# Block products at the openings of three networks and for the mixer's first eight units of a two-layer encoder trunk

## The chip, the cores and the metric

One Trainium2 chip, one core. A single launch computes the whole trunk. The metric is device time in microseconds (us), lower is better; the median of the runs counts.

The engines of a core run side by side: TensorE (PE) multiplies into PSUM, VectorE (DVE) and ScalarE (ACT) work elementwise, GpSimd (POOL) does a few elementwise operations and issues the DMAs that add in flight, and SyncE (SP) issues the plain loads. Each engine takes its instructions in order, and an instruction waits until the others have made what it needs.

## The reference

Two layers on 528 tokens (16 learned ones and 512 frames) of 1024 channels, all float32:

```python
for l in range(DEPTH):                       # 2
    h = h + 0.5 * swiglu(rmsnorm(h, g1[l]), w_gate1[l], w_up1[l], w_down1[l])   # 1024 -> 2816 -> 1024
    h = h + hybrid_mixer(rmsnorm(h, gm[l]), ...)
    h = h + 0.5 * swiglu(rmsnorm(h, g2[l]), w_gate2[l], w_up2[l], w_down2[l])
h = rmsnorm(h, final_norm)[:, N_META:]

def swiglu(x, wg, wu, wd): return (silu(x @ wg) * (x @ wu)) @ wd

def hybrid_mixer(u, ...):
    q, k, v, a, b, g_sb, g_conv = split(u @ w_in)     # 512 each, the gates 1024 each
    y_sb   = stick_breaking_attention(q, k, v) @ w_attn_out
    y_conv = silu(layernorm(depthwise_conv31(a * sigmoid(b)))) @ w_conv_out
    return (sigmoid(g_sb) * y_sb + sigmoid(g_conv) * y_conv) @ w_out
```

## The kernel before

Channels lie on the 128 partitions and tokens along the row: h is eight tiles of 128 x 528. To keep float32 accuracy every operand is a pair of a rounded high part and a low remainder, and every product is three matmuls: high by high, high by low, low by high. Tokens go as two halves of 264 (256 each where layer 1 has dropped the learned tokens, which the code calls XO).

**Units.** `units` (L130 on) lists the weight tiles in the order of use. A plain unit is one 128-column tile of a matrix, 8 blocks of 128 x 128: 8 x 3 x 2 = 48 matmuls. `unit` (L243) hands out the next and prepares three ahead (`LOOK`); `prep_unit` (L213) makes the pair `wh`, `wl`, four buffers of each. A network's tile is split by an ACT cast and a DVE subtraction (`split`, L77). A mixer's tile is cast on ACT, its negative written on ACT, and the low part made by a DMA that adds the weights once more (L224 to L226, POOL's queue). `fetch` (L179) loads raw tiles over SP's queue into three `wr` buffers, in the order of `fetches`.

**Block products.** Inside the networks most row pairs (m, m+1) of gate and up go by Strassen-Winograd (`quad`, L566): the 2 x 2 blocks of weights (two output rows by two halves of the channels) and of activations (two halves of the channels by two halves of the tokens) take seven products instead of eight, named w11, s1, s2, w21, s3, w22, s4. Each is 24 matmuls for gate and up together. The sums of weight blocks are loaded into `s1` and `s3` by a plain load and an adding DMA (`fetch_sums`, L196); s2 and s4 come out of s1 by one DVE addition (L236). The sums of activation blocks, `S[0]` to `S[3]`, come from `sums` (L365): two ACT copies, four DVE operations of half width, and two splits. The first three are made in the stage before (`prepare`, L313), the fourth in the head. Partial results are copied in PSUM (L599, L603) and subtracted by DVE (L608, L613).

**A network** (`ffn`, L467) opens with plain units, because its norm and the last sum are late: `head` (L517) does rows 0 and 1, four plain units, with the norm's matmuls (L409) inside the second; layer 0's first network has its own opening (`first_head`). Then quads and, in four groups, the down products (L260), which update h; the last group also makes the next stage's operands.

**A mixer** (`mixer`, L678) copies h to DRAM, then does units b and a in turn for four channel tiles (L761 to L774): b times the norm into a sigmoid, a times the norm, and their product `uc` on POOL. Products q, k, v and the gates follow (L720), with the attention between them. The causal convolution is 31 taps for each channel tile on DVE (L748), all of tile 0, then all of tile 1, and so on. `conv_some` puts them behind evictions at a late priority, two or four at a time; the last must be done before the layer norm's matmul (L1032), which stands behind the first attention-out unit (`AO_FIRST`).

Of the kernel before, what the change touches and what calls it, by code (L numbers as in the profile page):

```python
# [24 lines left out]
PLAIN, PLAIN_FIRST = 2, 4  # L25
# [8 lines left out]
CONV_STEP = 4  # L34
# [4 lines left out]
AO_FIRST = 1  # L39
# [21 lines left out]
def kernel(ctx, tc, hT, par, const, wg1, wu1, wd1, win, wao, wco, wout, wg2, wu2, wd2, out):  # L61
# [15 lines left out]
    def split(x, hi, lo):  # L77

        act.copy(hi, x)  # L79
        dve.tensor_tensor(out=lo, in0=x, in1=f(hi), op=ALU.subtract)  # L80

# [14 lines left out]
    def fn(out, in_, func, **kw):  # L96
# [8 lines left out]
        table["acts"].append(i)  # L105

# [3 lines left out]
    RAW_OF = {"w11": (0, 0), "w22": (1, 1), "w12": (0, 1), "w21": (1, 0)}  # L110
# [19 lines left out]
    units = []  # L130
    for l in range(DEPTH):
        for fi, (wg, wu, wd) in enumerate(((wg1, wu1, wd1), (wg2, wu2, wd2))):
            if fi == 1:
                for i in range(4):
                    units += [(("b", l, i), win[l, 16 + i], 8), (("a", l, i), win[l, 12 + i], 8)]
# [11 lines left out]
            m = PLAIN if l or fi else PLAIN_FIRST  # L147
            for m in range(m):
                units += [((f"g{fi}", l, m), wg[l, m], 8), ((f"u{fi}", l, m), wu[l, m], 8)]
            m += 1  # L150
# [8 lines left out]
    ready, raws, spared = {}, {}, set()  # L159
    quads = {"pool": None, "of": None}  # L160

    def pieces(n, block=None):

        key, src, nk = units[n]
        if nk in QUAD:
            wg, wu, m = src
            k, c = RAW_OF[block or nk]
            return [(4 * e, 4 * e + 4, w[m + c, :, 4 * k:4 * k + 4]) for e, w in enumerate((wg, wu))]
# [3 lines left out]
    fetches = []  # L172
    for n, (key, src, nk) in enumerate(units):
        if nk == "w11":
            fetches += [n, n + 5, n + 3]
        elif nk not in QUAD:
            fetches.append(n)

    def fetch(spare=None):  # L179

        while state["fetch"] < len(fetches) and (spare or state["out"] < RAW):
            n = fetches[state["fetch"]]
            state["fetch"] += 1
            if spare:
                raw = spare
                spared.add(units[n][0])
            else:
                state["out"] += 1
                raw = wpool.tile([P, 8, P], F32, tag="wr", bufs=RAW, name="wr")
            for a, b, src in pieces(n):  # L190
                nc.sync.dma_start(raw[:, a:b], src)
            raws[units[n][0]] = raw
            if spare:
                return

    def fetch_sums():  # L196

        n = state["sums"]
        while n < len(units) and units[n][2] != "w11":
            n += 1  # L200
        if n == len(units) or units[n][0][1:3] != quads["of"]:
            return
        state["sums"] = n + 1
        _, *at = units[n][0]
        for name, first in (("s1", "w11"), ("s3", "w22")):
            t = quads["pool"].tile([P, 8, P], F32, tag=name, bufs=2, name=name)
            for a, b, src in pieces(n, first):
                nc.sync.dma_start(t[:, a:b], src)
            for a, b, src in pieces(n, "w12"):
                pool.dma_start(t[:, a:b], src, accum_op=ALU.add)  # L210
            raws[(name, *at)] = t

    def prep_unit():  # L213
# [7 lines left out]
        if nk not in QUAD:  # L221
            raw = raws.pop(key)
            if key[0] in MIXER:
                act.copy(hi[:, :nk], raw[:, :nk])  # L224
                act.activation(lo[:, :nk], raw[:, :nk], AF.Copy, scale=-1.0)
                pool.dma_start(lo[:, :nk], src[:, :nk].bitcast(F32R), accum_op=ALU.add)  # L226
            else:
                split(raw[:, :nk], hi[:, :nk], lo[:, :nk])
            state["out"] -= key not in spared
        else:  # L230
            at = key[1:]
            if nk == "w11":
# [4 lines left out]
            split(raws[("s1" if nk in ("s2", "s4") else nk, *at)], hi, lo)  # L237
            for d in DONE[nk]:
                del raws[(d, *at)]
                state["out"] -= d in RAW_OF  # L240
# [36 lines left out]
    cc = cst.tile([P, N_CONST], F32, name="cc")  # L277
    ident = cc[:, C_ID:C_ID + P]
# [9 lines left out]
    def constants():  # L288

        nc.sync.dma_start(prm[:, N_NORM:], par[:, N_NORM:])  # L290
        nc.sync.dma_start(cc, const)
        with priority(LATE):
            dve.tensor_copy(trir, cc[:, C_TRI:C_TRI + P])
            dve.tensor_copy(l4, cc[:64, C_L4:C_L4 + P])
            dve.tensor_copy(l4[:, 95:96], cc[:64, C_L4 + 2 * P - 1:C_L4 + 2 * P])
# [853 lines left out]
```

## Time and profile before

| | |
|---|---|
| median of 3 runs | 2152.31 us |
| lowest and highest | 2151.03 and 2152.36 us |
| profiled execution, first to last instruction (span) | 2150.5 us |
| mean granted TensorE clock | 0.999 |
| DMA, mean | 151 GB/s, 324.90 MB |

The profile names a group of instructions by line, engine, operation and tile (out<-in), with its count, its busy time and the mean of one in ns, and then the idle time of the engine just before it and what ended that. The chain of waits is followed back from the last instruction; its rows are start and length in us. A row of busy time by window gives, for a stretch of the span, the busy time of each engine with the count of instructions in brackets. The profile's own time outside the span is not given; the median of the runs lies 1.8 us above it.

### The profile page before, as it was taken

The page shows a single profiled execution, that of the slowest core. Times are in us where ns is not written, and L with a number is a line of the kernel's source. Part 1 is how long each engine was busy: PE and PEld are TensorE (multiplying, and loading weights), DVE is VectorE, ACT ScalarE, POOL GpSimd, SP SyncE. Part 2 cuts the span into 40 slices and gives each one's busy share as a digit, 9 for nine tenths or more (in the row PEclk, how much of TensorE's full clock was granted, in tenths as well). Part 3 has the DMA queues.
Part 4 walks back from the last instruction along what each step waited for, and adds up shares of the span by engine and source line. Part 5 has one row for each costly group of instructions (what it writes and reads, how often), then busy time and mean ns, then how long its engine had stood idle before and what let it go on. Part 6 is the DMA issues. An engine that isn't in the chain of part 4 may idle for free.

```text
span 2150.5 us, 39932 instructions
## 1 busy us (share of the span) xinstructions
PE 2135.9 (99%) x16226; PEld 2052.8 (95%) x16226; DVE 1521.5 (71%) x2091; ACT 1137.9 (53%) x1587; POOL 488.7 (23%) x449
## 2 busy tenths in 40 slices
PE   9999999999999999999999999999999999999998
PEld 9999999999999999999999999999888889999897
DVE  7867685677766777677877676856677767767685
ACT  6434355467776545343554443554778775444354
POOL 1322321211111131313113223212112111322320
PEclk9999999999999999999999999999999999999999
DMA  8465536865578747464365655368656886665542
GB/s 236 133 165 141 142 104 198 181 138 119 134 169 180 175 129 189 129 161 122 99 169 145 168 140 146 103 193 184 142 127 133 187 188 167 159 175 143 144 111 77
DMA packets 140168, 324.90 MB, mean 151 GB/s; under 512 B 15568, under 2 KB 19664, under 8 KB 139984
## 3 DMA queue, kind: packets, MB, share of 16 engines
q1 hardware_dynamic: 101856, 226.36, 33.3%
q0 software_dynamic: 37440, 95.44, 26.1%
q8 instruction: 127, 2.08, 0.4%
q10 hardware_dynamic: 688, 0.55, 0.1%
q14 instruction: 57, 0.47, 0.1%
HBM read 315.86 MB, written 6.42 MB: 150 GB/s over the span
## 4 chain that ended last, share of the span: by engine, by line
PE 99%; ACT 0%; DVE 0%; DMA 0%; issue 0%; DVEq 0%; ACTq 0%
PE pb L580 16%; PE ps L580 16%; PE ps L720 15%; PE ps L260 12%; PE ps L706 10%; PE pe L260 6%; PE pb L260 6%; PE pe L580 5%; PE z L706 2%; PE ps L502 2%; PE pe L502 1%; PE pb L502 1%; PE z L877 1%; PE po L921 1%; PE z L900 1%; PE ps L554 1%
## 5 line engine op out<-in xcount | busy, mean ns | idle before, releaser
L79 ACT CAST wh<-wr 128x1024 fp32r<-128x1024 f32 (+4 forms) x275 | 242.2, 887 | 372.4 <-PE ps L260 94.5
L80 DVE TENSOR_TENSOR wl<-wr,wh 128x1024 fp32r<-128x1024 f32 (+4 forms) x275 | 300.6, 1096 | 57.4 <-ACT wh L79 53.5
L79 ACT CAST wh<-s 128x1024 fp32r<-128x1024 f32 x158 | 165.8, 1049 | 274.9 <-DVE s L236 83.1
L80 DVE TENSOR_TENSOR wl<-s,wh 128x1024 fp32r<-128x1024 f32 x158 | 216.1, 1368 | 59.4 <-ACT wh L79 58.7
L720 PE MATMUL ps<-uh,wh 128*128 128x264 f32 (+1 forms) x792 | 243.8, 308 | 0.0
L720 PE MATMUL ps<-uh,wl 128*128 128x264 f32 (+1 forms) x792 | 240.0, 303 | 0.0
L720 PE MATMUL ps<-ul,wh 128*128 128x264 f32 (+1 forms) x792 | 239.9, 303 | 0.0
L640 POOL TENSOR_TENSOR h<-h,dt 128x528 f32<-128x528 f32 (+1 forms) x96 | 179.9, 1879 | 258.1 <-DVE dt L638 255.2
L210 POOL DMA_DIRECT2D s<-wg x78 | 72.8, 938 | 596.9 <-DMA s<-wg 337.9
L748 DVE SCALAR_TENSOR_TENSOR y<-uc,prm,y 128x528 f32<-128x528 f32 (+1 forms) x240 | 197.7, 824 | 4.1
L224 ACT CAST wh<-wr 128x1024 fp32r<-128x1024 f32 x104 | 109.1, 1049 | 141.2 <-issue 46.9
L580 PE MATMUL ps<-ul,wh 128*128 128x264 f32 (+1 forms) x624 | 177.4, 284 | 0.0
L580 PE MATMUL pb<-sl,wh 128*128 128x264 f32 (+1 forms) x624 | 176.9, 283 | 0.0
L580 PE MATMUL ps<-uh,wl 128*128 128x264 f32 (+1 forms) x624 | 176.9, 283 | 0.0
L580 PE MATMUL pb<-sh,wl 128*128 128x264 f32 (+1 forms) x624 | 176.8, 283 | 0.0
L580 PE MATMUL pb<-sh,wh 128*128 128x264 f32 (+1 forms) x624 | 176.5, 283 | 0.0
L580 PE MATMUL ps<-uh,wh 128*128 128x264 f32 (+1 forms) x624 | 176.2, 282 | 0.0
L720 PEld LDWEIGHTS ps<-uh,wl 128*128 128x128 f32 x792 | 149.1, 188 | 5.9
L720 PEld LDWEIGHTS ps<-uh,wh 128*128 128x128 f32 x792 | 148.9, 188 | 5.4
L720 PEld LDWEIGHTS ps<-ul,wh 128*128 128x128 f32 x792 | 149.0, 188 | 5.1
L260 PE MATMUL ps<-ah,wh 128*128 128x264 f32 (+1 forms) x616 | 142.0, 300 | 0.0
L260 PE MATMUL ps<-ah,wl 128*128 128x264 f32 (+1 forms) x616 | 141.8, 300 | 0.0
(319 smaller groups left out, 6460.8 us busy)
## 6 DMA issues: line engine op xcount, KB each, us to landing
wr<-wd SPq DMA_DIRECT2D x96, 384.0 KB, 3.6
wr<-win SPq DMA_DIRECT2D x72, 512.0 KB, 4.4
wl<-win POOLq DMA_DIRECT2D x72, 512.0 KB, 7.8
wr<-wg SPq DMA_DIRECT2D x117, 256.0 KB, 3.0
wr<-wu SPq DMA_DIRECT2D x117, 256.0 KB, 3.4
s<-wg SPq DMA_DIRECT2D x78, 256.0 KB, 5.2
s<-wu SPq DMA_DIRECT2D x78, 256.0 KB, 5.7
s<-wg POOLq DMA_DIRECT2D x78, 256.0 KB, 5.2
```

Source lines behind the costliest of these rows:

```text
L79: act.copy(hi, x)
L80: dve.tensor_tensor(out=lo, in0=x, in1=f(hi), op=ALU.subtract)
L210: pool.dma_start(t[:, a:b], src, accum_op=ALU.add)
L224: act.copy(hi[:, :nk], raw[:, :nk])
L260: pe.matmul(ps[:, c, :n], wt[:, k0 + k, :], xt[:, s:s + n], start=(k == 0 and pi == 0), stop=(k == end and pi == 2))
L502: pe.matmul(ps[:, e, :TH], wt[:, k, :], xt[:, s], start=(k == ORDER[0] and pi == 0), stop=(k == ORDER[-1] and pi == 2))
L554: pe.matmul(ps[:, e, :TH], wt[:, k, :], xt[:, s], start=(k == 0 and pi == 0), stop=(k == KD - 1 and pi == 2))
L580: pe.matmul(ps[:, e, :TH], wt[:, 4 * e + kk, :], xt, start=start and kk == 0 and pi == 0, stop=kk == 3 and pi == 2, skip_group_check=True)
L640: pool.tensor_tensor(out=tri(h[j], mode), in0=tri(h[j], mode), in1=tri(t, mode), op=ALU.add)
L706: pe.matmul(ps, wt[:, k0 + k, :], xt[:, s], start=(n == 0 and pi == 0), stop=(n == nk - 1 and pi == 2))
L720: pe.matmul(ps, wt[:, k, :], xt[:, s], start=(n == 0 and pi == 0), stop=(n == KD - 1 and pi == 2))
L748: t = dve.scalar_tensor_tensor(out=y, in0=uc[i][:, c0 + k:k + T], scalar=col(w0 + k), in1=y, op0=ALU.mult, op1=ALU.add)
```

## The change

Layer 0's second network and both of layer 1's open with two row pairs, (0, 1) and (2, 3), both by block products, where rows 0 and 1 were plain. In the mixers the eight units b and a become two such pairs (b in the place of gate, a in that of up; channel tiles 0 and 1, then 2 and 3). The two pairs are interleaved in a fixed order; the first product of each, `o11`, leaves out its last channel block until both have done the rest. Layer 0's first network keeps its opening.

```diff
-PLAIN, PLAIN_FIRST = 2, 4
+PLAIN_FIRST = 4
-CONV_STEP = 4
+URGENT = 200
+CONV_STEP = 5
-AO_FIRST = 1
+AO_FIRST = 2
+    OPENING = (("o11", 0), ("o11", 1), ("o21", 0), ("s1", 0), ("s2", 0), ("o21", 1), ("w22", 0), ("s3", 0), ("s1", 1),
+               ("s4", 0), ("s2", 1), ("s3", 1), ("w22", 1), ("s4", 1))
...
-                for i in range(4):
-                    units += [(("b", l, i), win[l, 16 + i], 8), (("a", l, i), win[l, 12 + i], 8)]
+                units += open_pair((2, l), [(win[l, 16:20], win[l, 12:16], m) for m in (0, 2)])
...
+            if l or fi:
+                units += open_pair((fi, l), [(wg[l], wu[l], m) for m in (0, 2)])
```

In the openings `o11` and the first `o21` get their low part by an adding DMA, as a mixer's units do; the second `o21` is split on DVE. The first pair's s1 is loaded into a `wr` buffer (plain load and adding DMA), the other sums into tiles of the stage. s3's cast is held behind the Exp of the norm.

```diff
+    def pair(ptile, sp, st, mode, of, ats, between, take, done):
...
+        As = [ptile() for _ in range(2)]
+        ws = [unit("o11", *of, at) for at in ats]
+        for ks in (range(KH - 1), (KH - 1,)):
+            for A, w in zip(As, ws):
+                products(A, w, x(0, 0), True, ks)
+        Bs = [ptile("pb")]
+        begin(Bs[0], v(As[0]))
+        between(ptile("pe"), copies[0])
+        Bs.append(kept(As[1]))
+        def step(name, n):
+            w = unit(name, *of, ats[n])
+            if name == "o21":
+                products(As[n], w, x(0, 1))
+                take(n, As[n], 0, 0)
+            elif name == "s1":
+                G = ptile() if n else ptile("pe")
+                products(G, w, sx(0), True)
+                q[n] = kept(G)
+            elif name == "s2":
+                if n:
+                    keep, Bs[n] = Bs[n], ptile()
+                    begin(Bs[n], keep)
+                products(Bs[n], w, sx(1))
+                E[n] = ptile("pe")
+                opposite(E[n], Bs[n], q[n])
+            elif name == "s3":
+                products(Bs[n], w, sx(2))
+                c22[n] = sp.tile([P, 2, TH], F32, tag="c22", bufs=2, name="c22")
+                opposite(c22[n], Bs[n], q[n])
+                take(n, c22[n], 1, 1)
+            elif name == "w22":
+                products(E[n], w, sx(3))
+                take(n, E[n], 1, 0)
+            else:
+                done(n, 1)
+                products(Bs[n], w, x(1, 1))
+                take(n, Bs[n], 0, 1)
+                done(n, 0)
+        for name, n in OPENING[2:]:
+            step(name, n)
```

`between` makes the norm and the fourth sum of activation blocks, whose splits are held behind the first copy. `opposite` is the subtraction, in two half-width operations. Copies, subtractions and the norm get a higher priority (`URGENT`). `take` evicts: in a network into gate and up of half the tokens, with the splits for the down product in `done`; in a mixer as the sigmoid and the product, in halves.

In the mixer, the channel tiles' taps now go by turns within a pair, and may start when both tiles of the pair are complete:

```diff
-            todo = [(i, k) for i in range(4) for k in range(TAPS)]
+            todo = [(i, k) for p in (0, 2) for k in range(TAPS) for i in (p, p + 1)]
-                    while n and todo and todo[0][0] < len(uc):
+                    while n and todo and (todo[0][0] | 1) < len(uc):
...
-                for i in range(4):
-                    outs = gemm_b(None, unit("b", l, i), 0, KD, u, FULL)
...
-                    for out in by_halves(psp, FULL, "a", l, i):
...
+                    pair(btile, glu, st, FULL, (2, l), (0, 2), between, take, done)
```

The constants of the attention are loaded at the opening of layer 0's mixer instead of in the first network, and their tile lives there only. For the mixers' sums, the last down group of layer 0's and layer 1's first network now passes `alloc` on to `prepare`, so that it makes `S[0]` to `S[2]`:

```diff
-        ffn(l, 0, st, FULL, lambda tp, j, _: prepare(tp, j, base + KD, st1))
+        ffn(l, 0, st, FULL, lambda tp, j, alloc: prepare(tp, j, base + KD, st1, FULL, alloc))
```

249 lines of the change are left out of this document (170 added, 79 removed).

## The prediction

> **What bounds the kernel now.** I read the page's head first, then TensorE's list of waits, then the chain of waits.
>
> ```profile
> span 2150.5 us, 39932 instructions
> PE 2135.9 (99%) x16226; PEld 2052.8 (95%) x16226; DVE 1521.5 (71%) x2091; ACT 1137.9 (53%) x1587; POOL 488.7 (23%) x449
> ...
> PE ps L554 <- ACT wh L79: 4.8, 1, 4.8
> PE z L924 <- ACT vb L862: 0.2, 1, 0.2
> ...
> 49.78 5.85 PE pe L502 x48
> 730.48 5.85 PE pb L502 x48
> 754.38 5.83 PE ps L580 x48
> 363.97 4.36 PE pe L260 x36
> 368.33 5.83 PE z L706 x48
> 374.65 5.85 PE ps L720 x48
> 1811.20 5.64 PE pe L502 x48
> 1816.84 5.68 PE ps L580 x48
> ```
>
> TensorE waits 5.0 us in all, and only 4.8 at the very start, which the change leaves alone. The rest of the span is matmuls back to back, so the time is their count by their cadence. A row of the chain gives it: 48 matmuls of 264 columns take 5.83 us, 121.5 ns each. Plain units (L502, L706, L720: two halves under one weight tile) and block products (L580: a new weight tile for each matmul) go at the same pace; PE and PEld both count 16226, so a weight load stands before every matmul already. With 256 columns (layer 1's second network) the pace is 5.68 / 48 = 118.3 ns.
>
> **What the change removes.** Four plain units are 4 x 48 = 192 matmuls; the seven block products in their place are 7 x 24 = 168. So 24 go per two row pairs. Three networks lose one such group each: 24 x 121.5 ns = 2.92 us twice and 24 x 118.3 ns = 2.84 us once. Each mixer's eight units b and a become two groups: 48 x 121.5 = 5.83 us, twice. Sum: 2 x 2.92 + 2.84 + 2 x 5.83 = **20.34 us**. The norm's four matmuls stay. With nothing lost the span is 2150.5 - 20.34 = 2130.2. The median of the runs, 2152.31, lies 1.8 us above that profiled span; I keep the 1.8, so 2132.0 is the time without new stalls. Nothing can come back below that but scatter, since no wait of TensorE stands in the stretches that are touched.
>
> What follows is what is put beside these matmuls, and whether it stays beside them.
>
> **VectorE.** The views are busy time by window and the groups by form.
>
> ```profile
> 196.00:216.50 20.50, 20.50 (x170) 20.50 (x169) 16.18 (x22) 10.85 (x16) 3.51 (x4) 1.00 0.74 181
> 730.30:774.80 44.50, 44.50 (x368) 44.50 (x367) 30.60 (x43) 21.82 (x32) 10.58 (x12) 1.00 0.75 178
> 368.30:415.00 46.70, 46.70 (x387) 46.70 (x386) 28.37 (x45) 23.61 (x27) 11.29 (x14) 1.00 0.87 199
> 333.30:368.30 35.00, 35.00 (x291) 35.00 (x290) 20.38 (x29) 21.43 (x30) 4.67 (x6) 1.00 0.69 208
> 1052.40:1087.60 35.20, 35.20 (x291) 35.20 (x290) 30.23 (x48) 23.63 (x37) 1.93 (x2) 1.00 0.38 118
> L236 DVE TENSOR_TENSOR s<-s,wr 128x1024 f32<-128x1024 f32 x78 | 112.4, 1441 | 0.9
> L608 DVE SCALAR_TENSOR_TENSOR pe<-pb,q 128x528 f32<-128x528 f32 x29 | 20.7, 715 | 17.7 <-PE pb L580 17.7
> L592 DVE TENSOR_TENSOR g<-ps,rstd 128x264 f32<-128x264 f32 x29 | 12.5, 433 | 19.1 <-PE ps L580 19.1
> L80 DVE TENSOR_TENSOR al<-up,ah 128x528 fp32r<-128x528 f32 x66 | 46.4, 703 | 20.2 <-ACT ah L79 20.2
> L748 DVE SCALAR_TENSOR_TENSOR y<-uc,prm,y 128x528 f32<-128x528 f32 x120 | 101.4, 845 | 1.8
> ```
>
> The columns after the span are PE, PEld, DVE, ACT, POOL busy, the clock, DMA share and GB/s. A steady quad (first row) holds DVE 16.2 of 20.5 us. An opening is two quads, 32.4, plus its head: update, split and square sum of the last h (3 x 0.7), split of the sum (0.7), the fourth block sum (4 half-width operations at about L592's 0.43 and 2 splits x 0.7 = 3.1), the rsqrt (4 x 0.7 = 2.8): 8.7. The subtractions in halves add four times 2 x 0.433 - 0.715 = 0.6; one more add of weights falls inside the stretch, 1.2; the last pair's splits fall behind it, -1.4. That is 41.5 us, against 336 + 4 matmuls, 41.3 us, of TensorE: VectorE is full through an opening of a network, where in the same place it was 30.6 of 44.5. What covers it: units are prepared three ahead, 3 x 2.92 = 8.8 us, of which cast and subtraction use about 3, so a lag of some 5 us reaches no matmul, and the steady quads behind give 4 us each back. The nearest rows for the cost are nothing (the steady quad, no wait) and the whole excess of VectorE if it cannot run denser than now: I take **0.4 us** for each of the three, bounds 0 and 1.5. In a mixer the splits of the next units are DMA's work and nothing is split for a down product; 36 us plus 15 taps of 0.78 (0.845 with its overlap) overflow only in taps, whose order lies behind all else.
>
> Layer 0's and layer 1's first networks now make three block sums in their last down group: 3 x 3.1 = 9.3 us on 20.4 of 35.0, 29.7. The fifth row is a tail that already does this, at 30.2 of 35.2, with TensorE unbroken: cost 0.
>
> The new wait "behind the copies" holds the split of the fourth sum behind the ACT copy of A0; behind it in ACT's queue stand casts not due for 3 us. The wait "behind the norm" holds s3's cast behind the Exp; s3 is used 20.9 us into an opening. Both cost 0; without that cover, a copy, 0.6.
>
> **Transfers.** Next are the DMA table, then ACT's, SP's and POOL's time lines.
>
> ```profile
> q1 hardware_dynamic: 101856, 226.36, 33.3%
> q0 software_dynamic: 37440, 95.44, 26.1%
> ...
> 733.58 0.33 SPq L208 DMA_DIRECT2D s<-wg  x1
> 739.35 0.87 POOL L210 DMA_DIRECT2D s<-wg  x1 [29.38 <-DMA s<-wg]
> 747.67 1.05 ACT L79 CAST wh<-s 128x1024 fp32r<-128x1024 f32 x1 [6.36 <-DMA s<-wu]
> ...
> 357.08 0.33 SPq L191 DMA_DIRECT2D wr<-win  x1
> wr<-win SPq DMA_DIRECT2D x1, 512.0 KB, 4.7
> 361.72 0.87 POOL L226 DMA_DIRECT2D wl<-win  x1 [3.49 <-ACT wl L225]
> wl<-win POOLq DMA_DIRECT2D x1, 512.0 KB, 8.2
> 366.07 0.86 POOL L226 DMA_DIRECT2D wl<-win  x1 [3.48 <-ACT wl L225]
> wl<-win POOLq DMA_DIRECT2D x1, 512.0 KB, 8.4
> ...
> cc<-const SPq DMA_DIRECT2D x1, 392.0 KB, 7.7
> 370.04 0.72 ACT L318 ACTIVATE uh<-h,prm 128x528 fp32r<-128x528 f32 x1
> 372.88 0.71 DVE L80 TENSOR_TENSOR nt<-nsum,nt 128x528 fp32r<-128x528 f32 x1 [0.70 <-ACT nt L79]
> ```
>
> Plain loads move 226.36 MB in 33.3% of the span, 316 GB/s; accumulating ones 95.44 in 26.1%, 170 GB/s. An opening needs twelve plain loads of 0.524 MB (o11 and o21 four, s1 and s3 four, w22 and w21 four) and seven accumulating ones (o11, o11, the first o21, four sums): 19.9 + 21.6 = 41.5 us of DMA beside 41.3 of TensorE. So the queues too are full, where the mixer's old eight units, each one load of either kind, took 8 x (1.66 + 3.08) = 38 us of 46.7 (row: 0.87 with the copies of h).
>
> In a network behind a mixer this is early enough. Before, the first sum asked for at 733.58, 3.3 us after the opening began at 730.3, was fit to cast at 747.67, 17.4 us in, with three more sums in the same queue. Now s1 of the first pair is asked for about 15 us ahead, and s3 about at the opening; it must be cast by 17.9. Cost 0.
>
> A mixer comes behind units of 4.38 us and starts at T = 368.33. Three things are due earlier than today. The second unit's low half is issued at 361.72 and lands 8.2 us later, 369.9, T+1.6; the interleaved opening reads it behind 20 matmuls, T+2.4. Now two accumulations of s1 (asked for at 357.08, landing 4.7 later, 361.8) can stand ahead of it in POOL's queue, in order, at 0.9 each: T+3.4, a stall of **1.0 us**. The first o21, issued at 366.07, lands at 374.5, T+6.1, and is read at T+6.5: then covered by the same stall. And ACT's cast of s1, whose accumulation lands about T+2, can stand ahead of the last uh (370.04 now), and so put off the norm's operand, now there at 373.6, T+5.3, wanted at T+5.9 plus the stall. I take 1.0 for each mixer; bounds 0 (POOL takes the ready one first) and 3.6 (accumulation and norm both late). The constants move from the first network into layer 0's mixer, 0.4 MB or 1.3 us of SP's queue ahead of the sums there: in those bounds.
>
> **The convolution's end.** Taps by turns and steps of five leave 124 - 115 = 9 taps behind the attention, and the norm's matmul moves behind the second attention-out unit.
>
> ```profile
> 617.57 0.71 DVE L1016 TENSOR_TENSOR lsum<-lsum,y 128x528 f32<-128x528 f32 x1
> ...
> 625.97 0.77 DVE L726 TENSOR_TENSOR gs<-ps,gs 128x264 f32<-128x264 f32 x2 [2.10 <-PE ps L706]
> ...
> 628.82 1.05 PE L1032 MATMUL ps_ln<-lsum,ones 128*128 128x264 f32 x4
> ```
>
> Four last taps and three adds behind 625.97 are ready at 631.3; the norm then stands at 628.82 + 5.84 = 634.7. Cost 0, and 1 to 2 us a mixer if a tap is placed later.
>
> **Sum.** 2132.0 + 3 x 0.4 + 2 x 1.0 = **2135.2 us**.
>
> **Rivals.**
> 1. *The mixers' openings wait for accumulation and norm at the upper bounds.* For it: DMA is full there. Against: today's landings leave 0.8 us even with it full. 2 x 3.6 + 3 x 1.5 = 11.7: 2143.7, or 2139 to 2148. Chance 0.17.
> 2. *VectorE becomes the bound of the openings: slower than before.* Place: all five. If it runs there no denser than in a steady quad (16.2 / 20.5 = 0.79), 41.5 us of work take 52.5, 11.2 over TensorE; less the 5 that the lead absorbs, 6.2 each, 31 in all: 2163. It turns slower where each opening loses over 20.34 / 5 = 4.1. Against: DVE is idle in steady quads because it waits for TensorE (17.7 us ahead of L608, 19.1 ahead of L592 in the rows above). Chance 0.06.
> 3. *One long idle and a slow restart.* The row shows matmuls at the start of the program going at half pace.
>
> ```profile
> 5.00:10.00 5.00, 5.00 (x22) 4.88 (x23) 3.94 (x10) 4.39 (x11) 0.00 (x0) 1.00 1.03 338
> ```
>
> Here 22 matmuls fill 5.0 us, 227 ns, though the clock column says 1.00. A sum that comes 4 us late in each mixer, with 27 matmuls after it at 227 instead of 121.5 ns, costs 2 x (4 + 2.8) = 13.6: 2145.6. Chance 0.04. [...]
> 4. *The products do not save their seventh*, at a pace of 192 / 168 x 121.5 = 138.9 ns: no change, 2152. Against: L580 at 121.5 now. Chance 0.03.
>
> **How the numbers follow.** Forecast 0.70 (2131 to 2139), rivals 0.17, 0.06, 0.04, 0.03. The range 2131 to 2144 takes the forecast's bounds and most of rival 1, leaving out under 0.2. A measurement of this kernel can tell about 0.2%, 4.3 us: faster is below 2148.0. Faster: 0.70 + 0.17 + 0.04, less 0.02 for their upper ends, 0.89. Within: rival 4 and a part of 2, 0.06. Slower: the rest of 2, 0.05.
>
> **What would show it.** The page should count 16226 - 168 = 16058 matmuls, and the chain rows of 24 at 2.9 us in the openings. New waits of TensorE should be few, in the mixers, at the second unit's low half, the first o21 or the norm. DVE should be at 0.95 or more in the networks' openings. Waits of over 4 us in an opening, or a cadence above 122 ns there, would make the prediction wrong.

## The result, and the profile after

| | before | after |
|---|---|---|
| median (lowest to highest), us | 2152.26 (2151.03 to 2152.36) | 2186.07 (2183.72 to 2187.46) |
| after / before, 95% interval | | 1.0157 (1.0144 to 1.0171) |
| span of the profiled execution, us | 2150.5 | 2184.2 |
| mean granted TensorE clock | 0.999 | 0.990 |

The change makes the kernel 33.8 us slower, where the forecast was 17 us faster. First the page of the kernel after: span, busy times, and the shares of the chain that ended last.

```profile
span 2184.2 us, 40061 instructions
PE 2135.3 (98%) x16058; PEld 2047.1 (94%) x16058; DVE 1586.8 (73%) x2221; ACT 1183.1 (54%) x1672; POOL 534.4 (24%) x499
...
PE 89%; DMA 5%; DVE 3%; ACT 1%; issue 1%; SPq 0%; DVEq 0%; ACTq 0%; POOL 0%; POOLq 0%
```

The matmuls went from 16226 to 16058, as the change says, but the chain that was 99% TensorE now runs through DMA, VectorE and ScalarE for about a tenth of the span. TensorE's waits after (line, what it waited for, us in total, times, longest):

```profile
PE pe L443 <- DVE pe L461: 12.2, 3, 4.9
PE be L443 <- DVE be L461: 7.4, 2, 4.0
PE bs L443 <- DMA wl<-win: 5.2, 4, 2.2
PE ps L701 <- ACT wh L80: 5.0, 1, 5.0
PE ps L292 <- ACT wh L80: 2.7, 3, 0.9
PE bs L443 <- DVE be L461: 2.0, 2, 1.0
PE ps L443 <- DMA wl<-wg: 2.0, 1, 2.0
```

L443 is the products of an opening; L701 is the wait at the program's start that was there before. The first two rows are one wait in each of the five openings: w22 of the first pair waits for VectorE's difference E (L461). What VectorE did then, in layer 0's second network (VectorE's time line; in brackets its idle time and what ended it):

```profile
757.79 0.43 DVE L461 SCALAR_TENSOR_TENSOR pe<-pb,q 128x264 f32<-128x264 f32 x1
760.77 1.22 DVE L267 TENSOR_TENSOR wr<-wr 128x1024 f32<-128x1024 f32 x1 [2.55 <-DMA wr<-wu]
761.91 0.43 DVE L461 SCALAR_TENSOR_TENSOR pe<-pb,q 128x264 f32<-128x264 f32 x1
```

Between the two halves of E stands a weight addition (L267, s1 + w21, for a unit that comes later), and it waits for w21's load. The chain of waits, followed back from there:

```profile
752.08 0.33 SPq L207
...
752.45 8.23 DMA wr<-wu
...
760.77 0.13 DVE wr L267
...
761.91 0.44 DVE pe L461
```

The load is asked for at 752.08, when a raw buffer comes free, and takes 8.23 us to land. The same addition stands between the halves in all five openings. In the last one (layer 1's second network) s3 is late too: its accumulation takes 10.1 us to land, and VectorE waits for its cast ahead of E's first half.

```profile
1840.04 1.23 DVE L81 TENSOR_TENSOR wl<-s,wh 128x1024 fp32r<-128x1024 f32 x1 [5.00 <-ACT wh L80]
```

The openings by window, from the start of the first to the start of the last of their 336 products (us; PE, PEld, DVE, ACT, POOL busy; clock, DMA share, GB/s):

```profile
369.35:424.41 55.06, 47.37 (x341) 46.59 (x340) 39.22 (x62) 28.29 (x39) 15.17 (x19) 0.88 0.74 191
740.38:787.97 47.59, 42.98 (x343) 42.14 (x344) 36.41 (x56) 25.28 (x39) 12.18 (x14) 1.00 0.94 227
1100.92:1155.12 54.20, 47.04 (x346) 46.17 (x344) 38.03 (x59) 26.29 (x39) 12.36 (x14) 0.91 0.90 217
1467.54:1519.92 52.38, 45.17 (x342) 44.18 (x340) 38.85 (x59) 28.62 (x39) 15.27 (x18) 0.93 0.74 192
1820.69:1871.03 50.34, 44.18 (x340) 43.16 (x339) 36.88 (x57) 25.92 (x39) 12.25 (x14) 0.93 0.90 222
...
369.35:395.00 25.65, 21.43 (x150) 20.82 (x148) 17.38 (x30) 14.30 (x20) 6.72 (x11) 0.87 1.02 248
1467.54:1493.00 25.46, 19.26 (x151) 18.48 (x150) 19.08 (x28) 14.96 (x21) 6.43 (x9) 0.97 1.03 251
```

The five take 259.6 us in all. At the cadence of before (121.5 ns, 118.3 in the last) they would take 206.3: 339 steps in a mixer and the time of 343 in a network, where the norm's matmuls and the first few of a down product stand among the products. So 53.3 us were lost there, 28.2 in the networks and 25.1 in the mixers. Less the 20.3 that the products save, that is 33.0 of the 33.8 us of the result: next to nothing lies elsewhere. In the networks DMA is busy 0.90 to 0.94 of an opening, 45 to 49 us (47.59 x 0.94, 54.20 x 0.90); in the mixers it is full in the first 25 us (last two rows). VectorE is busy 36 to 39 us.

From one matmul's start to the next within these windows: gaps of over 150 ns beyond the cadence sum to 37.8 us ("stalls"), and matmuls at 1.6 to 2 times the cadence lose 15.0 us more ("half pace"). Of the stalls 21.3 are the ones at w22, 10.5 lie at the openings' starts, 6.0 at their ends. (The expectations below count slightly otherwise: 20.4 at w22, and 15.6 of half pace.)

### The profile page after: what moved, and what is told of

Read it like the earlier page. It is cut to its first block, busy times and chain, and to the rows that moved or that the text cites. A ratio compares the mean times of both kernels' runs of the same rounds, so it can differ in the third digit from the quotient of the medians.

```text
span 2184.2 us, 40061 instructions
## 1 busy us (share of the span) xinstructions
PE 2135.3 (98%) x16058; PEld 2047.1 (94%) x16058; DVE 1586.8 (73%) x2221; ACT 1183.1 (54%) x1672; POOL 534.4 (24%) x499
## 4 chain that ended last, share of the span: by engine, by line
PE 89%; DMA 5%; DVE 3%; ACT 1%; issue 1%; SPq 0%; DVEq 0%; ACTq 0%; POOL 0%; POOLq 0%
PE pb L725 14%; PE ps L725 14%; PE ps L861 13%; PE ps L292 11%; PE ps L847 10%; PE pb L292 5%; PE pe L292 5%; PE pe L725 5%; DMA wr<-wu 2%; PE ps L443 1%; DMA wr<-win 1%; PE z L1043 1%; PE bs L443 1%; PE po L1087 1%; PE pe L443 1%
## 5 line engine op out<-in xcount | busy, mean ns | idle before, releaser
L80 ACT CAST wh<-s 128x1024 fp32r<-128x1024 f32 x171 | 179.4, 1049 | 299.0 <-DVE s L267 85.8
L81 DVE TENSOR_TENSOR wl<-s,wh 128x1024 fp32r<-128x1024 f32 x171 | 233.0, 1362 | 52.5 <-ACT wh L80 50.1
L861 PE MATMUL ps<-uh,wh 128*128 128x264 f32 (+1 forms) x664 | 207.9, 313 | 0.3 <-DVE q L961 0.3
L861 PE MATMUL ps<-uh,wl 128*128 128x264 f32 (+1 forms) x664 | 203.6, 307 | 0.1
L861 PE MATMUL ps<-ul,wh 128*128 128x264 f32 (+1 forms) x664 | 203.7, 307 | 0.0
L725 PE MATMUL ps<-ul,wh 128*128 128x264 f32 (+1 forms) x576 | 163.7, 284 | 0.0
L725 PE MATMUL pb<-sl,wh 128*128 128x264 f32 (+1 forms) x576 | 163.3, 283 | 0.0
L725 PE MATMUL ps<-uh,wl 128*128 128x264 f32 (+1 forms) x576 | 163.3, 283 | 0.0
L725 PE MATMUL pb<-sh,wl 128*128 128x264 f32 (+1 forms) x576 | 163.2, 283 | 0.0
L725 PE MATMUL ps<-uh,wh 128*128 128x264 f32 (+1 forms) x576 | 162.6, 282 | 0.0
L292 PE MATMUL ps<-ah,wh 128*128 128x264 f32 (+1 forms) x616 | 142.7, 301 | 3.2 <-ACT wh L80 2.7
L292 PE MATMUL ps<-al,wh 128*128 128x264 f32 (+1 forms) x616 | 141.9, 300 | 0.5 <-DVE al L81 0.5
L292 PE MATMUL ps<-ah,wl 128*128 128x264 f32 (+1 forms) x616 | 141.7, 300 | 0.0
L861 PEld LDWEIGHTS ps<-uh,wl 128*128 128x128 f32 x664 | 125.0, 188 | 6.1 <-DMA wl<-win 0.3
L861 PEld LDWEIGHTS ps<-uh,wh 128*128 128x128 f32 x664 | 124.9, 188 | 6.2 <-issue 0.5
```

Of the source, the lines that this page charges most:

```text
L80: i = act.copy(hi, x)
L292: pe.matmul(ps[:, c, :n], wt[:, k0 + k, :], xt[:, s:s + n], start=(k == 0 and pi == 0), stop=(k == end and pi == 2))
L725: pe.matmul(ps[:, e, :TH], wt[:, 4 * e + kk, :], xt, start=start and kk == 0 and pi == 0, stop=kk == 3 and pi == 2, skip_group_check=True)
L861: pe.matmul(ps, wt[:, k, :], xt[:, s], start=(n == 0 and pi == 0), stop=(n == KD - 1 and pi == 2))
```

## The experiments

The kernel before was timed beside each (2151.5 to 2152.0); "openings", "stalls" and "half pace" are measured as above, in each run's own trace.

| kernel | us | ratio, 95% interval | openings | stalls | half pace |
|---|---|---|---|---|---|
| after | 2186.1 | 1.0157 (1.0144 to 1.0171) | 259.6 | 37.8 | 15.0 |
| e1 addition held | 2179.4 | 1.0127 (1.0112 to 1.0142) | 257.1 | 37.2 | 13.1 |
| e2 o11 split on VectorE | 2174.3 | 1.0106 (1.0091 to 1.0121) | 247.8 | 31.8 | 9.4 |
| e3 both | 2172.7 | 1.0097 (1.0082 to 1.0112) | 246.8 | 31.4 | 8.8 |
| f1 sums not accumulated | 2149.7 | 0.9991 (0.9982 to 1.0001) | 226.2 | 16.2 | 3.5 |
| f2 small additions | 2170.3 | 1.0085 (1.0070 to 1.0100) | 242.3 | 29.9 | 5.7 |
| f4 o11's low parts left out | 2171.0 | 1.0089 (1.0072 to 1.0106) | 245.8 | 29.8 | 9.2 |
| g1 sums loaded plainly | 2166.8 | 1.0070 (1.0053 to 1.0087) | 240.6 | 26.6 | 7.5 |
| j1 = f1 + f4 | 2148.1 | 0.9983 (0.9973 to 0.9992) | 223.8 | 14.0 | 3.3 |
| g2 = f1 + f2 + f4 | 2141.4 | 0.9953 (0.9938 to 0.9967) | 216.2 | 8.6 | 1.3 |
| h1 own buffer for w21 | 2178.4 | 1.0125 (1.0108 to 1.0142) | 250.0 | 33.3 | 9.7 |

### The first theory: one instruction in the wrong place

Theory A took the trace literally: the addition between the halves of E makes the stall. e1 holds it behind E, e2 takes the accumulating loads of o11 and the first o21 away and gives VectorE the subtractions instead, e3 does both, e4 puts the convolution's taps back in their old order.

```diff
# e1
-                dve.tensor_tensor(out=x, in0=x, in1=y, op=ALU.add)
+                add = dve.tensor_tensor(out=x, in0=x, in1=y, op=ALU.add)
+                if nk == "s4" and state.get("diff", (None,))[0] == tuple(at):
+                    tc.add_manual_dep(add.ins, state["diff"][1].ins.name, NOSYNC, reason="behind the difference")
...
# e2
-            if key[0] in MIXER or nk0 == "o11" or nk0 == "o21" and units[n - 1][2] == "o11":
+            if key[0] in MIXER:
# e4
-            todo = [(i, k) for p in (0, 2) for k in range(TAPS) for i in (p, p + 1)]
+            todo = [(i, k) for i in range(4) for k in range(TAPS)]
-                    while n and todo and (todo[0][0] | 1) < len(uc):
+                    while n and todo and todo[0][0] < len(uc):
```

> Edit: the weight addition s1 + w21 of an opening's pair (which becomes s4's operand) is held on VectorE behind the second half of that pair's last difference E. Theory A (VectorE, in order, stands still at that addition for w21's late load, and the half difference that w22 needs stands behind it; TensorE idles 3.5 to 5 us and then runs at half pace): the waits of w22 in the first pair of all five openings, 20.4 us in all, go nearly to nothing, and with them most of the half-pace matmuls, some 13 of 15.6 us: about 2153 us, between 2149 and 2160, mean granted clock at 0.997 or more. Theory B (VectorE or the transfers are simply full through an opening, whatever the order): the idle time turns up elsewhere in the same openings and the time stays at 2175 or more.

> Edit: the low parts of o11 and of the first o21 of an opening are made by VectorE's subtraction, as for other units of the networks, and not by an accumulating load. Theory A: the stalls at the starts of the two mixers' openings and of layer 1's first network (8.7 us with their half-pace part some 11) come from the order of POOL's queue, where the accumulations of s1 stand ahead of the second unit's low half; they go, the ones at w22 stay: 2172 to 2180 us. Theory B (VectorE full): its four further subtractions an opening, 1.2 us each, delay the first pair's differences by up to 5 us: no gain or slower, 2186 to 2200.

> Edit: both of the above. Theory A, as the causes are apart: 2186 less 33 less 10, so about 2143 us, between 2138 and 2152, with idle time left at the ends of the openings, about 1 us each. Theory B: 2170 or more.

> Edit: the convolution's taps in the old order, tile after tile, with the old condition for their start; everything else as changed, the steps of five and the attention's early outs too. Theory A (all of the loss lies in the openings): within 2 us of the changed kernel, 2184 to 2188. Rival C (taps that stand ahead of the openings' work on VectorE make the late differences): 5 us or more less, below 2181.

Measured: 2179.4, 2174.3, 2172.7 and 2185.8 (1.0159, 1.0142 to 1.0176). e4 says that the taps' order costs and gains nothing. e1 refutes theory A: 7 us, not 33, which is where theory B had it. e2, which adds three subtractions to an opening (not four, as its expectation says), came where theory A had it (2172 to 2180), but not for its reason: the stalls at the openings' starts only shrink from 10.5 to 6.3 us, while those at w22, which were to stay, shrink from 21.3 to 10.7. TensorE's waits of e1:

```profile
PE pb L445 <- DVE c L463: 9.0, 3, 3.8
PE bb L445 <- DVE c L463: 6.4, 2, 3.2
```

The stall at w22 is nearly gone in four openings (3.2 us are left in the last, where s3 is late) and has come back at the product s4, whose weights are s1 + w21. It waits for the other difference, c22 (L463), again behind late loads. In these runs an order of instructions only chooses where the lateness shows. e3 is hardly below e2, so the causes do not add up.

### Transfers or VectorE: leaving work out

Theory T: the transfers of an opening are too many for its time, whatever the order. Theory V: VectorE's work is. f1 and f4 take accumulating loads away and leave VectorE's work; f2 takes some 4 us of VectorE's work from each opening and leaves the transfers.

```diff
# f1, in fetch_sums (in fetch likewise)
-            load(t, n, "w11" if name == "s1" else "w22", "w12")
+            load(t, n, "w11" if name == "s1" else "w22", *(("w12",) if tuple(at) not in opened else ()))
# f2
+                b = 1 if at in opened else 8
+                dve.tensor_tensor(out=x[:, :b], in0=x[:, :b], in1=y[:, :b], op=ALU.add)
# f4
-                for a, b, src in pieces(n):
+                for a, b, src in pieces(n) if nk0 not in OPEN else ():
...
```

> Edit: the sums s1 and s3 of the openings' pairs are loaded without their accumulated second block, so four accumulating loads of 0.5 MB an opening are left out (the sums are then one block each); VectorE, ScalarE and TensorE do the same instructions. The held addition only moved the stall from w22 to w21's product, so theory A in its narrow form is out. Theory T (transfers: some 41 us of DMA are asked for in a burst of 20 us, and what is due in it, w21's and w22's blocks among it, lands late): the stalls at w22, w21 and at the openings' starts go for the most part, and with them the half pace: 2140 to 2155. Theory V (VectorE's work is too much for an opening): 2175 or more.

> Edit: the four weight additions of an opening on VectorE add only an eighth of their columns (so s2's and s4's operands are not the sums), which takes some 4 us of VectorE's work from each opening and leaves every wait and every transfer as it is. Theory T: 2180 to 2188. Theory V: 15 us or more less, below 2171.

> Edit: the accumulating loads that make the low parts of o11, o11 and the first o21 exact are left out (the low part is then the negated weight), so three accumulating loads an opening go, and VectorE gets nothing in their place; this is the experiment that split them on VectorE (2174) without that engine's work. Theory T: 2160 to 2170, as there is less to transfer, and the waits for the norm and the sums' splits that the split brought on VectorE are not there. Theory V says the same of these waits, and leaves the rest: 2160 to 2176. A time above 2172 would say that neither the queue nor VectorE's work at the openings' starts matters.

Measured: 2149.7, 2170.3, 2171.0. Both theories have their run: without four of an opening's accumulating loads 36 us come back, with VectorE's part all there, and with narrower additions 16. f4 decides nothing, since both theories had it near 2170. The 36 and the 16 us overlap, so the next runs were to separate them: all three together, and then the two on transfers alone, with VectorE's work whole.

> Edit: three leavings-out together: no accumulation in the openings' sums, none in the low parts of o11, o11 and the first o21, and the four weight additions an eighth as wide. TensorE's instructions are all there. If the openings' loss is all of transfers and of VectorE's line behind them, what is left is the 20.34 us that the products save and the stalls of about 1 us at the ends of the openings: 2135 to 2142. If 2146 or more, the change has another cost that these do not touch.

> Edit: two leavings-out together, without the third: no accumulation in the openings' sums (2149.7 alone) and none in the low parts of o11, o11 and the first o21 (2171 alone); VectorE's four additions of an opening are whole again. All three together gave 2141.4. Theory T (the transfers alone make the loss, and small additions gain because they stand in line behind late loads): 2140 to 2144, the same as all three. Theory T+V (VectorE's own work is a cost of its own): 2146 to 2150, with idle time of TensorE ended by VectorE in the openings' first pairs.

Measured: 2141.4 and 2148.1. The same five windows in j1:

```profile
368.52:412.60 44.08, 42.34 (x342) 41.57 (x340) 39.29 (x62) 28.02 (x39) 11.16 (x12) 1.00 0.54 160
728.53:773.30 44.77, 42.76 (x344) 42.10 (x344) 36.40 (x56) 25.34 (x39) 6.97 (x8) 1.00 0.73 192
1086.24:1131.72 45.48, 42.68 (x345) 42.03 (x344) 37.32 (x59) 26.12 (x39) 7.00 (x8) 1.00 0.73 195
1444.15:1487.60 43.45, 41.97 (x342) 41.37 (x340) 38.64 (x59) 28.37 (x39) 10.98 (x12) 1.00 0.50 154
1788.70:1834.71 46.01, 42.90 (x341) 41.90 (x339) 36.25 (x57) 25.69 (x39) 6.99 (x8) 0.96 0.71 188
```

VectorE's busy time is the same as after the change (36.40 and 36.41 us in the second row), the DMA share falls from 0.94 to 0.73 and the openings from 259.6 to 223.8 us. So the transfers carry 35.8 of the 53.3 us lost. The load that made the stall shows it directly. In j1 w21 is asked for 11.7 us into that opening, as it is after the change (740.23 and 752.08), but lands in 5.8 us instead of 8.23, and VectorE waits 1.52 us for it instead of 2.55:

```profile
740.23 0.33 SPq L207 DMA_DIRECT2D wr<-wg  x1
746.44 1.23 DVE L267 TENSOR_TENSOR wr<-wr 128x1024 f32<-128x1024 f32 x1 [1.52 <-DMA wr<-wu]
```

The narrower additions give 7.6 us more (223.8 to 216.2), where they gave 17.3 while the loads were late. This is what is left for VectorE's own work, and at most that, since a load still stops its line in j1. What waits in g2 is the openings' ends and the copies:

```profile
PE ps L293 <- ACT wh L80: 2.8, 3, 1.0
PE bs L444 <- DVE be L462: 2.0, 2, 1.0
...
PE ps L444 <- ACT pb L455: 0.9, 3, 0.3
```

g2 is 10.6 us faster than the kernel before. The products do save what they should; the openings' data come too late for it.

### Pace, amount, or the time of asking

g1 loads the second block of each sum plainly over the first. f3 and g3 put off the sums of the quad behind a network's opening; f3 only emitted them later in the program, g3 held them in SyncE's queue.

```diff
# g1: for the openings' sums
-        for queue, block, kw in zip((nc.sync, pool), blocks, ({}, {"accum_op": ALU.add})):
+        for queue, block, kw in zip((nc.sync, pool), blocks, ({}, {} if sums else {"accum_op": ALU.add})):
...
# f3
-            if nk == ("s1" if at in opened else "w11"):
+            if nk == ("s1" if at in opened and at[2] == 0 else "s4" if at in opened else "w11") and (nk != "s4" or at[2]):
# g3: f3, and in load()
+                if queue is nc.sync and behind:
+                    tc.add_manual_dep(i.ins, behind.ins.name, NOSYNC, reason="behind the opening")
...
```

> Edit: in the openings' sums the second block is loaded plainly over the first instead of being accumulated onto it: the same bytes, the same queues, the same order of one load behind the other, but no accumulation (the sums are then the second block alone). Leaving these accumulations out gave 2149.7, 36 less than the changed kernel. Theory T1 (the price is the accumulation's slow pace in a full DMA): most of that comes back, 2150 to 2162. Theory T2 (the price is that a second load exists and stands behind the first): 2175 or more.

> Edit: the sums s1 and s3 of the first quad behind a network's opening are asked for when the opening's last unit is prepared, not when the second pair's s1 is; nothing is left out. It takes 1 to 2 MB (some 5 to 10 us of DMA) out of the burst in the three networks that have an opening, and nothing in the mixers. Theory T: the stalls at w22 there (12.7 us and some 6 of half pace) shrink by half or more: 2168 to 2178. Theory V: 2183 or more.

> Edit: nothing left out. The earlier edit of this aim had no effect, since the queue still issued the first quad's sum at the same place (745.9 us, ahead of w21's load at 752.0). Now those loads are held in SyncE's queue behind the load of the opening's last w21. Theory T: 1 to 2 MB leave the burst of the three networks, the stalls at w22 there shrink by half: 2170 to 2180. If 2183 or more, the burst's size is not what makes w21's load late, but its own late request, 752.0 us, when a buffer comes free.

g1: 2166.8, between the two theories: 19 of f1's 36 us come with the accumulation, the rest with the second load itself. f3: 2185.5 (1.0158, 1.0143 to 1.0173), inconclusive, since SyncE's queue still issued the sum at 745.91, as after the change (745.98). g3: 2183.5 (1.0147, 1.0132 to 1.0162); now that sum is asked for at 763.24, and w21's load takes 7.99 us instead of 8.23. The DMA share of the first 22 us only falls from 0.98 to 0.96: other transfers fill the room. So is it the late request? h1 gives w21 a buffer of its own and asks for it at 739.34, 3.7 us into the opening instead of 11.7; h2 adds e2's split.

```diff
# h1, in fetch_sums
+        if names == ("s3",):
+            names = ("s3", "w21")
...
```

> Edit: nothing left out. The first pair's w21 of each opening gets a buffer of its own in the openings' pool, and is asked for right behind s3, when that pool opens (in layer 0's second network about 743 us), instead of waiting for the raw buffer that o21's split gives back (752.0 us, landed 760.7). In the mixers the constants pass through a raw buffer and tmp has two buffers instead of three, to make room. Theory L (the late request: w21's load comes too late since its buffer does, and VectorE's line stands behind it): the stalls at w22 and what they bring go for the most part, without giving the bytes back anywhere: 2155 to 2167. Theory D (the DMA is full, so an early request of w21 makes s3 and the second pair's sums late by as much): 2178 or more.

> Edit: nothing left out. The same, with the low parts of o11, o11 and the first o21 split by VectorE, which alone gave 2174. Theory L: about 10 us under the one with the own buffer alone, 2146 to 2157. Theory D: the split takes 1.5 MB of accumulating loads out of each opening, so what the own buffer could not gain alone it gains here in part: 2160 to 2172.

Measured: 2178.4, and 2173.6 (1.0109, 1.0093 to 1.0125) for h2: h1 is at the edge of theory D (2178 or more), h2 just above its range. The early request gains 7.7 us at most, and in h2 next to nothing over e2. The chain of h1 at the same stall:

```profile
740.31 5.65 DMA s<-wg
...
747.25 7.84 DMA s<-wu
...
755.19 1.05 ACT wh L80
...
756.26 1.23 DVE wl L81
757.49 0.36 DVE pe L463
...
757.99 0.36 PE pe L445
```

w21 is early now, and the sums are what VectorE's line waits for. The chain's two loads are the second pair's s1 (not s3, as k1's expectation has it): its plain load takes 5.65 us and its accumulation 7.84, and its split stands ahead of E's second half instead. s3's split stands ahead of the first half; its cast starts 16.4 us into the opening, where it started at 14.9 after the change. The full DMA (0.96 of this opening) passed the lateness on to the next operand. g4 shows it from the other side. It is e1 with the first pair's s1 accumulated behind the low parts of o11 and o21, which are due before it:

```diff
# g4: e1, and in prep_unit, behind the first o21's low part
+                if nk0 == "o21":
+                    n1 = n + 1
+                    for a, b, src in pieces(n1, "w12"):
+                        k = pool.dma_start(raws[units[n1][0]][:, a:b], src, accum_op=ALU.add)
+                        tc.add_manual_dep(k.ins, i.ins.name, NOSYNC, reason="behind the opening's units")
...
```

> Edit: nothing left out. The held addition (2179) and, in GpSimd's queue, the accumulation of the first pair's s1 put behind the low parts of o11 and o21, which are due before it. If the stalls at the openings' starts come from that queue's order: 8 to 10 us less than the held addition alone, 2167 to 2173. If DMA is simply full there, the late sum costs as much as the early one did: 2176 or more.

Measured: 2191.0 (1.0185, 1.0170 to 1.0201), 11.6 us over e1. The waits at the starts of the openings changed their name and grew:

```profile
PE be L541 <- ACT nt L80: 13.8, 2, 7.0
PE pe L541 <- ACT nt L80: 11.6, 3, 4.8
```

The norm's operand (nt) now waits in ScalarE's line behind the cast of the late s1.

### Orders and another engine

k1 makes each difference one instruction over both halves, so that nothing can stand between them; k2 adds e3 to it; k3 adds e2 and puts an opening's four weight additions on GpSimd.

```diff
# k1
-            for e in range(2):
-                with priority(-URGENT):
-                    dve.scalar_tensor_tensor(out=out[:, e, :TH], in0=c[:, e, :TH], scalar=-1.0, in1=q[:, e],
-                                             op0=ALU.mult, op1=ALU.add)
+            with priority(-URGENT):
+                return dve.scalar_tensor_tensor(out=v(out), in0=v(c), scalar=-1.0, in1=q, op0=ALU.mult, op1=ALU.add)
...
# k3
-                dve.tensor_tensor(out=x, in0=x, in1=y, op=ALU.add)
+                (pool if at in opened else dve).tensor_tensor(out=x, in0=x, in1=y, op=ALU.add)
```

> Edit: nothing left out. Each difference of an opening (E and c22) is one VectorE instruction over both halves instead of two, so that nothing that waits for a load can stand between the halves; with the own buffer for w21 it was the split of s3 that stood there. Theory T (what is short is transfers; the line only decides where it shows): 2176 to 2186, the idle time goes to s3's, w21's or the next unit's start. Theory O (VectorE's order makes the loss): 2160 to 2172.

> Edit: nothing left out. The same with the held addition and the low parts of o11, o11 and the first o21 split by VectorE (these two without whole differences: 2172.7). Theory T: 2167 to 2173. Theory O: 2152 to 2164.

> Edit: nothing left out. Whole differences, the split low parts, and the four weight additions of each opening on GpSimd instead of VectorE. Making these additions small gained 16 us. If that was their 1.2 us each on VectorE and the waits for loads in its line, most of it comes here too: 2155 to 2164. GpSimd's own additions take some 3.5 us each by its 528-column rows (1.6 to 1.9 us), ahead of the accumulating loads in its queue: if that decides, 2174 or more.

Measured: 2182.6 (1.0143, 1.0128 to 1.0158), 2175.5 (1.0106, 1.0089 to 1.0123) and 2183.1 (1.0145, 1.0130 to 1.0160). k1 is as theory T has it, k2 2.5 us above T's range and far from O's. In k1 TensorE's idle time goes to s4, as in e1 (10.4 and 8.4 us in its list of waits). k3 is where its expectation has it if GpSimd's own time decides (2174 or more). No order, with e2's split or without, recovers more than 14 of the 34 us. On GpSimd the additions took 2.6 to 2.7 us each, on VectorE 1.22 to 1.44, and its queue also issues the accumulating loads. No version with all of the work came under the kernel before.

## Why the prediction was wrong

**The removed matmuls** were right: 16058, and g2, which has them all, comes to 2141.4 against the 2132.0 that the sum gave without new stalls.

**Transfers: the step that failed.** "In a network behind a mixer this is early enough ... Cost 0." The step had worked out 41.5 us of DMA beside 41.3 of TensorE, and then priced only the landing of the sums, each by itself. That part held in layer 0's second network: s3 was asked for 2.7 us into the opening and its cast began at 14.9, where 17.9 was the limit. What it did not ask for are the plain blocks whose addition makes the next operand. w21 can only be asked for when a raw buffer comes free, 11.7 us in, and in the full DMA (a share of 1.09 while it was under way) it took 8.23 us. It landed 2.5 us after VectorE had come to that addition, and the half difference that w22 needs stands behind it. In layer 1's second network the sum was late as well (its cast began at 18.3). DMA was busy 45 to 49 us in a network's opening and not 41.5, since loads for the units behind fall into it too. In the mixers the 1.0 each covers only the start: their openings lost 13.9 and 11.2 us, mostly at w22 and in half pace. Taking the seven accumulating loads away gave 35.8 us back in the five openings, where the sum had 2.0 for transfers in the mixers and nothing in the networks.

**VectorE** was estimated at 41.5 us in a network's opening and measured 36 to 38, a share of 0.70 to 0.77 and not 0.95, so it was not full. The sum took the steady quad's row twice, with the eight subtractions for low parts that stand in that row's window. An opening has eleven, and three of half the width, since o11 and the first o21 get their low part from DMA, as the step on transfers itself counts; at 1.22 us each, 0.69 the narrow ones, that makes 15.5 us instead of 19.6. Its cost of 0.4 was still too small, for another reason. "The steady quads behind give 4 us each back" does not hold: behind an opening come the first down units, whose operands wait (L292, 2.7 us in three openings), and the line stops at each late load. What the narrower additions still give once the accumulating loads are gone, 7.6 us or 1.5 an opening, comes out at the step's upper bound.

**The mixers' starts** have the mechanism as forecast, the second unit's low half behind s1's accumulations, with the row "PE bs L443 <- DMA wl<-win" at 5.2 us in two mixers instead of 2.0. As forecast, too, s1's cast stands ahead of the last uh there (372.03 and 372.98) and the norm's operand behind it. Layer 1's first network, priced at nothing, has the same wait (2.0).

**Rival 2** had the size, not the cause: "52.5, 11.2 over TensorE" in each opening, where 53.3 / 5 = 10.7 were lost. That the two agree is chance: its 41.5 us of VectorE are not there, it named VectorE instead of DMA, and the 5 us that it took off for the lead of the units cannot be seen in the runs. **Rival 3** came as an addition: the half pace behind the stalls cost 15.0 us by itself. (Its 27 matmuls are those behind the 4.8 us wait at the start of the kernel before, nearly all 0.22 us apart.) **Rival 4** is out by g2. **The convolution's end** and **the tails** cost nothing, as forecast: TensorE's list has no wait there, and e4 is level with the kernel after.

What was to show the prediction wrong did: waits of over 4 us in openings. Two things remain open: how the transfers' share splits between their number and the accumulation's pace, for g1 gives about half to each, but it also changes the sums' landing; and how much of the last 17.5 us that j1 loses in its openings is VectorE's own work (at most the 7.6 that narrower additions gain).

## What to carry to other kernels

Where a stage's transfers come out at the stage's own length, price every load of the stage, not only the ones that look critical, with the landing times measured while DMA is full, and look at when buffers let each be asked for. A saving on the bounding engine that shortens the stage leaves less time for them. When a stalled engine stands behind an instruction that waits for a load, move that instruction once; if the stall turns up at the next operand with nothing gained, the order alone is not the cause, and leaving out a part of the transfers, and then a part of the engine's work, tells more.

## What the runs showed of the hardware

**Half pace followed four of five stalls, and not by their length alone.** Five stalls of the kernel after by window, each followed by the stretch behind it:

```profile
758.90:762.40 3.50, 0.29 (x3) 0.08 (x1) 1.63 (x3) 1.34 (x2) 0.00 (x0) 1.00 1.10 262
762.40:768.00 5.60, 5.51 (x45) 5.54 (x46) 4.61 (x7) 2.35 (x4) 0.86 (x1) 1.00 1.01 290
...
1103.20:1105.60 2.40, 0.40 (x4) 0.22 (x3) 2.02 (x3) 2.33 (x5) 0.00 (x0) 1.00 1.09 258
1105.60:1109.30 3.70, 3.70 (x18) 3.67 (x19) 3.67 (x7) 0.63 (x1) 0.00 (x0) 0.54 1.07 252
...
1123.00:1127.40 4.40, 0.45 (x4) 0.24 (x3) 1.68 (x3) 0.34 (x1) 0.00 (x0) 0.87 1.08 256
1127.40:1134.00 6.60, 6.56 (x33) 6.59 (x34) 4.50 (x6) 2.21 (x4) 1.76 (x2) 0.57 0.80 232
...
1488.90:1492.70 3.80, 0.38 (x4) 0.20 (x2) 1.77 (x3) 1.47 (x2) 0.00 (x0) 0.84 1.09 259
1492.70:1498.70 6.00, 6.00 (x29) 6.00 (x30) 4.73 (x7) 1.60 (x3) 1.45 (x1) 0.53 0.59 197
...
1838.70:1843.80 5.10, 0.29 (x3) 0.08 (x1) 3.47 (x5) 2.69 (x4) 0.78 (x1) 0.93 1.10 262
1843.80:1850.00 6.20, 6.11 (x29) 6.14 (x30) 4.68 (x6) 2.35 (x4) 0.86 (x1) 0.51 0.99 260
```

By the starts of the matmuls on either side, the stalls are 3.58, 2.28, 4.27, 3.70 and 5.19 us long; a matmul's own 0.28 us is part of that. After 3.58 us 45 matmuls fit into 5.6 us at a clock of 1.00. After 3.70 us only 29 fit into 6.0, at a clock of 0.53, and after 4.27 and 5.19 us 33 into 6.6 and 29 into 6.2, at 0.57 and 0.51. That loses a further 2.5 to 2.8 us each time (6.0 less 29 x 0.1215; 6.6 less 33 x 0.1215; 6.2 less 29 x 0.1183). After 2.28 us 18 fit into 3.7, at 0.54, another 1.5 us lost (3.7 less 18 x 0.1215). So 3.30 us of idle time left the pace alone, where 2.00 and 3.42 halved it; what decides it no run shows. In the four of half pace the cadence was back 3.7 to 6.1 us after the stall's end.

**An accumulating load landed 10.2 us after its issue, a plain one in its place 6.1.** From layer 0's second network: the DMA queues of the kernel after from 740.38 to 775 (packets, MB, share of the engines' time), then the second block of the second pair's s1, wu's part, from issue to landing (KB, us), after the change and in g1, where it is a plain load:

```profile
q0 software_dynamic: 1699, 3.09, 49.8%
q1 hardware_dynamic: 2779, 5.07, 45.9%
...
s<-wu POOLq DMA_DIRECT2D x1, 256.0 KB, 10.2
...
s<-wu POOLq DMA_DIRECT2D x1, 256.0 KB, 6.1
```

GpSimd's queue, which has the accumulating loads, moves 3.09 MB in half of the engines' time and SyncE's 5.07 in most of the other half; their sum, 95.7%, is what is full. The six such loads of this opening's three later sums land in 7.2 to 12.8 us after the change and in 4.7 to 6.9 in g1, from the same queue; g1's DMA is somewhat less full there too (0.86 of the opening instead of 0.94).

**GpSimd's additions took 2.6 to 2.7 us each, VectorE's 1.22 to 1.44.** These are the means of the 128 x 1024 additions in k3 and after the change (wr<-wr 1.22; s<-s,wr, with the quads', 1.44), where the expectation had 3.5 for GpSimd. Those of k3:

```profile
L267 POOL TENSOR_TENSOR wr<-wr 128x1024 f32<-128x1024 f32 x10 | 27.3, 2734 | 66.8 <-DVE wl L81 48.4 <-DMA wr<-wu 14.6 <-DMA wr<-win 3.7
L267 POOL TENSOR_TENSOR s<-s,wr 128x1024 f32<-128x1024 f32 x10 | 26.1, 2608 | 8.0 <-DMA wr<-wu 3.2 <-DVE wl L81 3.2 <-DVE g L644 1.6
```
